# Conditioning weights asked for in two pairs, and three more merge additions on VectorE, in a decoder layer on one Trainium2 core

## The chip, the cores and the metric

The kernel runs on one core of one Trainium2 chip. The metric is device time in microseconds (us): the median of 3 runs of the unchanged kernel is 1647.31 (1646.59 to 1651.67).

## What is computed

One layer of a hybrid decoder, for a prompt of 1024 tokens and 8 samples of 8 tokens (1088 columns together; features stand in the 128 partitions), all in float32. Cut to what matters here:

```python
sh, sc, gt = ada_mod(c, w_ada_mix, b_ada_mix)
h = rms_norm(x, norm_mix) * (1 + sc) + sh
P = h @ w_in                                   # 34 blocks of 128 columns
...
merged = g_r * (o_r @ w_br_rwkv) + g_p * (o_p @ w_br_pool)
x = x + gt * (merged @ w_out)
sh, sc, gt = ada_mod(c, w_ada_mlp, b_ada_mlp)  # silu(c) @ w + b
h = rms_norm(x, norm_mlp) * (1 + sc) + sh
x = x + gt * (square(relu(h @ w_ff1)) @ w_ff2)
y = rms_norm(x, norm_final)
```

## The kernel before

Every large product is done with split operands: a weight piece of 128 x 512 (256 KB, tile `wraw`) is loaded by the SyncE queue (SP), rounded by ScalarE to `whi` (L207), and VectorE or GpSimd in turn forms the rest `wlo` (L208). TensorE then does three matmuls per 128-row slice (`mm3`). Raw buffers are two, so a load waits until the split of the piece two before it is done; rounded pieces are four deep in the second phase.

The first phase (to about 778 us of the span) projects, runs the recurrent and the pooling branch and stores the pooled half of the merge in DRAM. The second phase (`phase2`) begins with eight **merge rows** m = 0 to 7 (`or_job`): the last 512 rows of the recurrent branch are multiplied by `w_br` in three chunks of columns (two in PSUM tiles `mm`, one in `w`), VectorE multiplies each with the gate (L1406, into tile `t`), then the pooled part `u` (in a buffer of the tag `hid`) is added over all 1088 columns (L1410): on GpSimd for rows 0 to 6, on VectorE for row 7. ScalarE rounds the two halves of the sum to `mr` (L1413) and VectorE splits off the rest (L1414). Row 7's sum is also the mark for which the next stage waits.

Then come the eight **output blocks** (`out_job`), first for the left half of the columns, then for the right: each takes two pieces of `w_out`, 24 matmuls of 272 columns apiece, and ends in a residual step on VectorE (L1964), a store `d_xr` (L1448) and a square on ScalarE (L1450) that VectorE sums up (L1452). Blocks 0 and 1 are interleaved, so that the first two pieces need only merge rows 0 to 3.

Beside the output blocks the **conditioning of the MLP** is computed (`ada` in `phase2`, `ada_part`): of `w_ada_mlp` three parts g, of which g = 0 and 1 fall into this stage. Each has two groups of four loads of 512 KB into the four `hid` buffers (L305, on SP); 16 narrow matmuls `wc<-hid` consume a group. After the second group ScalarE copies the sum to `asb` (L311) and eight small matmuls `wc<-kct,asb` spread it. Before the four tiles of the very first group stands a GpSimd copy each of one column of merge row 7's sum (`behind`, L1379), so that the loads don't start before that sum is there.

What sets the order: TensorE's order is written by hand, by a pace (`Pace`) that adds up estimated times; a generator's `yield n` asks to go on n ns of that pace later. The other engines and the queues are ordered by the language's scheduler. Each engine and queue works strictly in its order, and a wait holds up all that stands behind it.

Of the kernel before, what the change touches and what calls it, by code (L numbers as in the profile page):

```python
# [13 lines left out]
ALU = mybir.AluOpType  # L14
# [136 lines left out]
class K:  # L151
# [144 lines left out]
    def ada_part(self, name, g, tile_of, sb, dst, bias, blocks, gap, turn=2000, lead=0, n=1):  # L296

        nc = self.nc
        ps = self.ps("wc")
        for k2 in range(0, 4, n):  # L300

            ws = []
            for i in range(2 * n):
                ws.append(tile_of())
                nc.sync.dma_start(ws[i], self.io[name][2 * k2 + i, g])  # L305
            yield gap if k2 else gap + lead
            for i in range(2 * n):
                for h in range(2):
                    q, k = 64 * (i % 2) + 32 * h, 2 * k2 + i
                    self.mm(ps[q:q + 32, :], self.sT[:, k, :], ws[i][:, h * 512:(h + 1) * 512], start=k < 2, stop=k > 5, tile_position=(0, q))  # L310
        nc.scalar.activation(sb, ps, AF.Copy)  # L311
        yield turn
        po = self.ps("wc")
        for i in range(4):
            self.mm(po[:, i * 18:(i + 1) * 18], sb[:, i * 128:(i + 1) * 128], self.kc("sel"), start=True, stop=True)
        b0, step = blocks[0], blocks[1] - blocks[0]
        pick = lambda t: t.rearrange("p (g h b) q -> p g h b q", h=2, b=4)[:, b0 // 8] if step == 4 else t.rearrange("p (h b) q -> p h b q", b=8)[:, 0:2, b0:b0 + 4]
        bb = pick(self.part[:, PC[bias]:PC[bias] + 24].unsqueeze(2))
        nc.vector.tensor_tensor(pick(dst), po[:, :72].rearrange("p (b h q) -> p h b q", h=2, q=9), bb.to_broadcast([P, 2, 4, 9]), op=ALU.add)
# [1046 lines left out]
    def phase2(self):  # L1366

        nc, io, p = self.nc, self.io, self.p2
# [8 lines left out]
        def behind(x):  # L1377

            nc.gpsimd.tensor_copy(x[:, 0:1], self.mark[:, 0:1])  # L1379
            return x  # L1380
# [17 lines left out]
        def or_job(m):  # L1398
            S = {}

            def begin():
                t, S["u"] = T(), self.row(p, "hid", 4)
                S["t"] = t
                nc.scalar.dma_start(t, self.d_th[m])
                nc.scalar.dma_start(S["u"], self.d_th[8 + m])
                return lambda c0, n, ps: nc.vector.scalar_tensor_tensor(t[:, c0:c0 + n], t[:, c0:c0 + n], 1.0, ps[:, :n], op0=ALU.add, op1=ALU.mult)  # L1406

            def after():
                t = S["t"]
                (nc.vector if m == 7 else nc.gpsimd).tensor_tensor(t, t, S["u"], op=ALU.add)  # L1410
                hi, lo = zip(*[MR() for _ in range(2)])
                for i, s in enumerate(split):
                    nc.scalar.activation(hi[i], t[:, s], AF.Copy)  # L1413
                    nc.vector.tensor_tensor(lo[i], t[:, s], hi[i].bitcast(F32), op=ALU.subtract)  # L1414
                mg[0].append(hi)
                mg[1].append(lo)
                self.mark = t
                self.xr.append(HX(F32))
                nc.gpsimd.dma_start(behind(self.xr[m]), io["xT"][m])
                self.done.add(("or", m + 4))  # L1420

            return Job([io["w_br"][m][:, 0:512]], begin, after=after, xs=lambda: orr, tags=TG)
# [672 lines left out]
```

## Time and profile before

| | |
|---|---|
| median of 3 runs | 1647.31 us |
| profiled execution | 1653.89 us, its span 1652.1 us |
| mean granted TensorE clock | 0.987 |
| merge rows and output blocks | about 778 to 945 us of the span |

The profile gives busy time by engine (PE is TensorE, PEld its weight loads, DVE VectorE, ACT ScalarE, POOL GpSimd, SP SyncE), and rows in order of time: start, length, engine, line, operation, tile written <- tiles read, shape and count; in brackets the idle time of the engine before it, and what ended it. A queue is marked by a q (SPq). DMA rows give the time of issuing, not of landing. The chain that ended last is the path of work and waits followed back from the end.

### The profile page before, as it was taken

How to read it: one execution, taken by the hardware profiler on the slowest of the kernel's cores; microseconds unless marked ns; L12 is line 12 of the kernel's file. 1: busy time of each engine (PE TensorE's matmuls, PEld its weight loads, DVE VectorE, ACT ScalarE, POOL GpSimd, SP SyncE). 2: the span in 40 equal slices, each digit the busy share in tenths (PEclk: the TensorE clock that was granted, in tenths of full speed). 3: DMA queues.
4: the chain of work that ended last, by engine and by line, in shares of the span. 5: the costliest groups of instructions: out<-in, count | busy, mean ns of one | idle time of the engine just before them, and what ended most of it. 6: DMA issues, size and time to landing. Idle time of an engine off the chain costs nothing.

```text
span 1652.1 us, 35483 instructions
## 1 busy us (share of the span) xinstructions
PE 1598.5 (97%) x14331; PEld 1492.5 (90%) x14331; DVE 1019.8 (62%) x1744; ACT 738.9 (45%) x1491; POOL 365.9 (22%) x467
## 2 busy tenths in 40 slices
PE   6999999999998999999989999999999999999997
PEld 3989888887897889889979999999999999999997
DVE  5675655745665456434543696777545677776866
ACT  4443343344334433423223475555444665553323
POOL 3300200010001000101621332323223342521221
PEclk9989999999999999999999999999999999999999
DMA  9324313314332323564875355666656965564213
GB/s 334 113 103 137 133 62 110 117 54 139 100 114 76 121 93 119 220 223 153 327 266 203 131 181 182 226 232 238 227 205 216 345 205 188 199 245 180 99 39 109
DMA packets 123332, 279.43 MB, mean 169 GB/s; under 512 B 16768, under 2 KB 31104, under 8 KB 123168
## 3 DMA queue, kind: packets, MB, share of 16 engines
q1 hardware_dynamic: 107808, 228.52, 39.6%
q0 software_dynamic: 9312, 32.41, 5.8%
q10 hardware_dynamic: 6048, 16.23, 2.7%
q8 instruction: 113, 1.85, 0.4%
q14 instruction: 51, 0.42, 0.1%
HBM read 198.15 MB, written 78.95 MB: 168 GB/s over the span
## 4 chain that ended last, share of the span: by engine, by line
PE 61%; ACT 2%; DVE 2%; DMA 2%; issue 1%; POOL 1%; SPq 0%; DVEq 0%; POOLq 0%; ACTq 0%
PE pr L184 32%; PE mm L184 21%; PE w L184 6%; PE wc L184 2%; DMA wraw<-in_w_out 1%; DVE hx L1772 0%; DMA wt<-d_x 0%; POOL t L1410 0%; PE w L191 0%; ACT whi L207 0%; DVE hx L1941 0%; POOL wr L1745 0%; ACT mr L1695 0%; ACT hx L1695 0%; DMA wraw<-in_w_ff 0%
## 5 line engine op out<-in xcount | busy, mean ns | idle before, releaser
L184 PE MATMUL mm<-hx,whi 128*128 128x362 f32 (+1 forms) x1920 | 510.0, 347 | 0.6 <-ACT px L551 0.6
L184 PEld LDWEIGHTS mm<-hx,whi 128*128 128x128 f32 x1920 | 333.3, 191 | 34.4 <-issue 17.1
L184 PE MATMUL pr<-mr,whi 128*128 128x272 f32 x1792 | 336.2, 287 | 0.3 <-DVE hx L1772 0.3
L184 PE MATMUL mm<-hx,wlo 128*128 128x362 f32 (+1 forms) x960 | 316.1, 329 | 0.0
L184 PEld LDWEIGHTS pr<-mr,whi 128*128 128x128 f32 x1792 | 280.7, 188 | 2.1 <-issue 1.3
L184 PE MATMUL pr<-mr,wlo 128*128 128x272 f32 x896 | 257.8, 288 | 0.0
L207 ACT ACTIVATE whi<-wraw 128x512 fp32r<-128x512 f32 x186 | 116.8, 629 | 217.9 <-PE mm L184 60.4
L184 PEld LDWEIGHTS mm<-hx,wlo 128*128 128x128 f32 x960 | 183.1, 191 | 0.0
L208 DVE TENSOR_TENSOR wlo<-wraw,whi 128x512 fp32r<-128x512 f32 x145 | 110.6, 764 | 116.5 <-ACT whi L207 114.0
L184 PE MATMUL pr<-hx,whi 128*128 128x272 f32 x896 | 168.8, 287 | 1.8 <-DVE rs L1967 0.8
L184 PEld LDWEIGHTS pr<-mr,wlo 128*128 128x128 f32 x896 | 168.6, 188 | 0.0
L184 PE MATMUL mm<-mr,whi 128*128 128x272 f32 (+4 forms) x736 | 154.3, 304 | 1.6 <-DVE t L1406 1.6
L184 PEld LDWEIGHTS pr<-hx,whi 128*128 128x128 f32 x896 | 140.3, 188 | 3.3 <-ACT whi L207 1.0
L207 ACT ACTIVATE whi<-wr 128x512 fp32r<-128x512 f32 x138 | 86.5, 628 | 117.3 <-PE pr L184 80.5
L184 PE MATMUL pr<-hx,wlo 128*128 128x272 f32 x448 | 128.9, 288 | 0.0
L184 PEld LDWEIGHTS mm<-mr,whi 128*128 128x128 f32 x736 | 120.7, 191 | 4.8 <-issue 2.5
L184 PE MATMUL mm<-mr,wlo 128*128 128x272 f32 (+4 forms) x368 | 111.0, 302 | 0.0
L208 POOL TENSOR_TENSOR wlo<-wraw,whi 128x512 fp32r<-128x512 f32 x41 | 54.8, 1336 | 216.3 <-ACT whi L207 216.3
L208 DVE TENSOR_TENSOR wlo<-wr,whi 128x512 fp32r<-128x512 f32 x103 | 77.2, 752 | 16.6 <-ACT whi L207 16.6
L184 PE MATMUL pr<-t,whi 128*128 128x272 f32 x448 | 84.6, 287 | 0.0
L184 PEld LDWEIGHTS pr<-hx,wlo 128*128 128x128 f32 x448 | 84.3, 188 | 0.0
L184 PEld LDWEIGHTS pr<-t,whi 128*128 128x128 f32 x448 | 70.2, 188 | 0.8 <-issue 0.8
(400 smaller groups left out, 2714.9 us busy)
## 6 DMA issues: line engine op xcount, KB each, us to landing
wr<-in_w_ff SPq DMA_DIRECT2D x137, 256.0 KB, 3.3
hid<-d_ch POOLq DMA_DIRECT2D x72, 272.0 KB, 3.7
wraw<-in_w_ff SPq DMA_DIRECT2D x71, 256.0 KB, 3.1
wraw<-in_w_in SPq DMA_DIRECT2D x68, 256.0 KB, 2.9
d_ch<-hx SPq DMA_DIRECT2D x52, 272.0 KB, 3.6
hid<-in_w_ada_mlp SPq DMA_DIRECT2D x24, 512.0 KB, 6.4
d_th<-px SPq DMA_DIRECT2D x22, 544.0 KB, 3.0
wt<-d_x SPq DMA_DIRECT2D x20, 544.0 KB, 4.2
```

What stands on the lines that cost most here:

```text
L184: return self.nc.tensor.matmul(out, lhsT, rhs, **kw)
L207: nc.scalar.activation(hi, raw, AF.Copy)
L208: (nc.gpsimd if pool else nc.vector).tensor_tensor(lo, raw, hi.bitcast(F32), op=ALU.subtract)
```

## The change

There are two edits. In `ada_part` a group of four loads (n = 2) is asked for in two pairs, with half of the gap between them, and the wait after the second pair is shorter by that half. Groups with n = 1 are as before. In `or_job` the addition of `u` is on VectorE for rows 4 to 7, where it was on VectorE for row 7 alone.

```diff
             ws = []
             for i in range(2 * n):
+                if i == 2:
+                    yield gap // 2
                 ws.append(tile_of())
                 nc.sync.dma_start(ws[i], self.io[name][2 * k2 + i, g])
-            yield gap if k2 else gap + lead
+            yield (gap if k2 else gap + lead) - (gap // 2 if n > 1 else 0)
...
             def after():
                 t = S["t"]
-                (nc.vector if m == 7 else nc.gpsimd).tensor_tensor(t, t, S["u"], op=ALU.add)
+                (nc.vector if m > 3 else nc.gpsimd).tensor_tensor(t, t, S["u"], op=ALU.add)
```

In the changed kernel all lines from L304 on stand two lower (L1410 is L1412, L207 and L208 stay).

**VectorE, merge rows 4 to 6.** `t_9045`, `t_9107`, `t_9169` and `t_9231` are rows 4, 5, 6 and 7; `mr` are their split halves; `wlo_9215` belongs to a piece of `w_out`. Before, from the end of row 5 to row 7:

```order
L1406 SCALAR_TENSOR_TENSOR t_9169<-t_9169,mm_9173 128x364
L1414 TENSOR_TENSOR mr_9160<-t_9107,mr_9160 128x544
L1406 SCALAR_TENSOR_TENSOR t_9169<-t_9169,mm_9174 128x362
L1406 SCALAR_TENSOR_TENSOR t_9169<-t_9169,w_9175 128x362
L1414 TENSOR_TENSOR mr_9161<-t_9107,mr_9161 128x544
L208 TENSOR_TENSOR wlo_9215<-wraw_9212,whi_9214 128x512
L1414 TENSOR_TENSOR mr_9222<-t_9169,mr_9222 128x544
L1406 SCALAR_TENSOR_TENSOR t_9231<-t_9231,mm_9235 128x364
L1406 SCALAR_TENSOR_TENSOR t_9231<-t_9231,mm_9236 128x362
L1414 TENSOR_TENSOR mr_9223<-t_9169,mr_9223 128x544
```

The same place in the changed kernel:

```order
L1416 TENSOR_TENSOR mr_9160<-t_9107,mr_9160 128x544
L1416 TENSOR_TENSOR mr_9161<-t_9107,mr_9161 128x544
L1408 SCALAR_TENSOR_TENSOR t_9169<-t_9169,mm_9173 128x364
L1408 SCALAR_TENSOR_TENSOR t_9169<-t_9169,mm_9174 128x362
L1408 SCALAR_TENSOR_TENSOR t_9169<-t_9169,w_9175 128x362
L1412 TENSOR_TENSOR t_9169<-t_9169,hid_9170 128x1088
L1416 TENSOR_TENSOR mr_9222<-t_9169,mr_9222 128x544
L1416 TENSOR_TENSOR mr_9223<-t_9169,mr_9223 128x544
L208 TENSOR_TENSOR wlo_9215<-wraw_9212,whi_9214 128x512
L1408 SCALAR_TENSOR_TENSOR t_9231<-t_9231,mm_9235 128x364
L1408 SCALAR_TENSOR_TENSOR t_9231<-t_9231,mm_9236 128x362
L1408 SCALAR_TENSOR_TENSOR t_9231<-t_9231,w_9237 128x362
```

The addition L1412 is new in VectorE's order, and a row's work is now closed before the next row's products begin; the split of a weight piece stands behind both halves of row 6.

**SP, from the second group of conditioning loads on.** `hid` are conditioning loads, `wraw` pieces of `w_out`, `d_xr` stores of a finished output block. Before:

```order
L196 DMA wraw_9483<-in_w_out 128x512
L305 DMA hid_9472<-in_w_ada_mlp 128x1024
L305 DMA hid_9474<-in_w_ada_mlp 128x1024
L305 DMA hid_9476<-in_w_ada_mlp 128x1024
L305 DMA hid_9478<-in_w_ada_mlp 128x1024
L196 DMA wraw_9513<-in_w_out 128x512
L196 DMA wraw_9551<-in_w_out 128x512
L1448 DMA d_xr_122<-hx_8980 128x544
L196 DMA wraw_9581<-in_w_out 128x512
L196 DMA wraw_9628<-in_w_out 128x512
L1448 DMA d_xr_123<-hx_9042 128x544
L305 DMA hid_9651<-in_w_ada_mlp 128x1024
```

And in the changed kernel:

```order
L196 DMA wraw_9479<-in_w_out 128x512
L307 DMA hid_9472<-in_w_ada_mlp 128x1024
L307 DMA hid_9474<-in_w_ada_mlp 128x1024
L196 DMA wraw_9509<-in_w_out 128x512
L307 DMA hid_9541<-in_w_ada_mlp 128x1024
L307 DMA hid_9543<-in_w_ada_mlp 128x1024
L196 DMA wraw_9551<-in_w_out 128x512
L1450 DMA d_xr_122<-hx_8980 128x544
L196 DMA wraw_9581<-in_w_out 128x512
L196 DMA wraw_9628<-in_w_out 128x512
L1450 DMA d_xr_123<-hx_9042 128x544
L196 DMA wraw_9670<-in_w_out 128x512
```

One piece of `w_out` now stands between the two pairs of this group, and one more stands ahead of the third group (as one does ahead of the fourth). In the first, third and fourth group the four loads still follow one another.

**ScalarE, around `asb`.** `whi` are rounded pieces of `w_out`, `t_9595` is the square of output block 3. Before:

```order
L207 ACTIVATE whi_9515<-wraw_9513 128x512
L207 ACTIVATE whi_9553<-wraw_9551 128x512
L1450 ACTIVATE t_9595<-hx_9042 128x544
L207 ACTIVATE whi_9583<-wraw_9581 128x512
L311 ACTIVATE asb_9298<-wc_9299 128x512
```

And in the changed kernel:

```order
L207 ACTIVATE whi_9511<-wraw_9509 128x512
L207 ACTIVATE whi_9553<-wraw_9551 128x512
L207 ACTIVATE whi_9583<-wraw_9581 128x512
L1452 ACTIVATE t_9595<-hx_9042 128x544
L313 ACTIVATE asb_9298<-wc_9299 128x512
```

The square and the third rounding have changed places; `asb` stands behind both as before.

## Prediction

> **What bounds the kernel now.** I read the page first, then the windows by stage, then the list of who waited for whom, then the order of time around each wait that TensorE (PE) shows.
>
> ```profile
> span 1652.1 us, 35483 instructions
> PE 1598.5 (97%) x14331; PEld 1492.5 (90%) x14331; DVE 1019.8 (62%) x1744; ACT 738.9 (45%) x1491; POOL 365.9 (22%) x467
> ```
>
> PE is busy for 97% of the span and VectorE (DVE) for 62%. A change that touches DVE, GpSimd (POOL) and the SyncE queue (SP) can therefore only gain where PE stands still, or lose where it makes PE stand still. The change sits in the merge and output stage, 778 to 945 us. The waits of PE from 700 to 960, and three windows there (columns: width, busy of PE, PEld, DVE, ACT, POOL, then granted clock, DMA share, GB/s):
>
> ```profile
> PE wc L184 <- ACT asb L311: 2.9, 1, 2.9
> PE mm L184 <- DVE t L1406: 1.6, 1, 1.6
> PE pr L184 <- DVE rs L1967: 0.8, 1, 0.8
> PE wc L184 <- DVE t L1452: 0.5, 1, 0.5
> ...
> 830.00:840.00 10.00, 10.00 (x81) 10.00 (x81) 7.03 (x11) 3.31 (x6) 4.31 (x8) 1.00 0.76 284
> ...
> 860.00:870.00 10.00, 7.09 (x36) 6.92 (x35) 2.90 (x6) 3.02 (x5) 1.27 (x1) 0.66 0.93 340
> ```
>
> Four waits, two of them large. After the 1.6 us one the clock stays at 1.00. Around the 2.9 us one only 36 matmuls run in 10 us and the granted clock is 0.66, so that wait costs more than its length. TensorE's rows at the two places, and four pieces of the chain that ended last, for the usual pace:
>
> ```profile
> 827.93 0.29 PE L184 MATMUL mm<-mr,wlo 128*128 128x272 f32 x1
> 829.84 0.49 PE L184 MATMUL mm<-mr,whi 128*128 128x272 f32 x2 [1.61 <-DVE t L1406]
> ...
> 859.88 0.29 PE L184 MATMUL mm<-mr,wlo 128*128 128x272 f32 x1
> 863.08 1.89 PE L184 MATMUL wc<-kct,asb 128*128 128x18 f32 x8 [2.91 <-ACT asb L311]
> 864.80 0.80 PE L184 MATMUL mm<-mr,whi 128*128 128x272 f32 x2
> ...
> 869.03 0.47 PE L184 MATMUL mm<-mr,whi 128*128 128x272 f32 x2
> ```
> ```profile
> 811.35 0.49 PE w L184 x3
> 811.84 1.00 PE mm L184 x6
> ...
> 897.64 0.80 PE wc L184 x8
> ...
> 902.08 31.39 PE mm L184 x252
> ```
>
> The usual pitch of a 272-column matmul is 31.39/252 = 0.125 us. **Place A:** from 827.93 + 0.125 to 829.84 PE loses 1.78 us. **Place B:** from 859.88 + 0.125 to 863.08 it loses 3.08. The eight small matmuls then take 864.80 - 863.08 = 1.72 instead of 0.80, 0.92 more; and the 18 matmuls between 864.80 and 869.03 (six groups of three) take 4.23 instead of 18 x 0.125 = 2.24, 1.99 more. B is 5.99 us, of which 2.91 is the slow clock. A and B together are 7.77 us.
>
> **What ends the wait at A.**
>
> ```profile
> 824.86 2.94 POOL L1410 TENSOR_TENSOR t<-t,hid 128x1088 f32<-128x1088 f32 x1
> 825.33 3.02 DVE L208 TENSOR_TENSOR wlo<-wraw,whi 128x512 fp32r<-128x512 f32 x1
> 828.52 0.73 DVE L1414 TENSOR_TENSOR mr<-t,mr 128x544 fp32r<-128x544 f32 x1 [0.17 <-ACT mr L1413]
> 829.16 0.97 DVE L1406 SCALAR_TENSOR_TENSOR t<-t,mm 128x364 f32<-128x364 f32 x2
> ...
> 831.98 1.29 DVE L1410 TENSOR_TENSOR t<-t,hid 128x1088 f32<-128x1088 f32 x1
> ```
>
> Merged row 6's addition runs on POOL until 827.80. DVE has the split of row 6 in its order ahead of the gated products of row 7 (L1406), so the two PSUM banks that the second output block needs come free only at 829.7. Besides, the weight split at 825.33 took 3.02 us, against 0.69 in a row below, and ended just after that addition. [...] The same addition on DVE (row 7, 831.98) took 1.29, less than half of POOL's 2.94.
>
> **Edit 2, the additions of rows 4 to 6 on DVE.** Row lengths for the schedule:
>
> ```profile
> 812.08 0.52 DVE L1406 SCALAR_TENSOR_TENSOR t<-t,w 128x362 f32<-128x362 f32 x1
> ...
> 816.35 0.72 DVE L1414 TENSOR_TENSOR mr<-t,mr 128x544 fp32r<-128x544 f32 x1 [3.12 <-ACT mr L1413]
> ...
> 818.96 0.69 DVE L208 TENSOR_TENSOR wlo<-wraw,whi 128x512 fp32r<-128x512 f32 x1
> ```
> ```profile
> 815.66 1.21 ACT L1413 ACTIVATE mr<-t 128x544 fp32r<-128x544 f32 x2 [4.79 <-POOL t L1410]
> ```
>
> By the new DVE order a row is: three products (about 0.45 apart, 1.4), addition 1.29, wait for ScalarE's first half (816.35 - 815.66 = 0.69), two splits (0.65 apart, 1.35), in two rows of three one weight split (0.69): 4.7 to 5.4 us. PE's row is 36 matmuls at (0.49 + 1.00)/9 = 0.165, 5.94 us, so DVE keeps up. Row 4's last product ends at 812.60 as before (row 3 still waits for POOL). From there: one split left, addition to 814.5, its splits to 816.5; row 5's products to 817.9, addition 819.1, weight split and splits 821.2; row 6's products 822.5, addition 823.8, splits 825.8, weight split 826.5; row 7's first product 827.0, last 827.9, addition 829.2. The first product of row 7 is then 2.7 us earlier than now, and 1.1 before PE wants it at 828.05: A goes. POOL still has two weight splits of 1.3 in this time (the chain's row at 857.68); if each held DVE up for 0.7, A keeps 0.3. I take 1.5 of A's 1.78 as gained.
>
> The addition of row 7 ends at 829.2 instead of 831.98 + 1.29 = 833.27: **4.1 us earlier**. Four POOL copies wait for it, and the first conditioning loads wait for those copies.
>
> **What ends the wait at B, and edit 1.** The SP queue, then the chain, then ScalarE and DVE:
>
> ```profile
> 834.06 1.77 SPq L305 DMA_DIRECT2D hid<-in_w_ada_mlp  x4
> 836.23 0.86 SPq L196 DMA_DIRECT2D wraw<-in_w_out  x2
> 837.19 2.79 SPq L1448 DMA_DIRECT2D d_xr<-hx  x2
> 846.36 0.33 SPq L196 DMA_DIRECT2D wraw<-in_w_out  x1
> 846.78 1.91 SPq L305 DMA_DIRECT2D hid<-in_w_ada_mlp  x4
> 848.79 2.15 SPq L196 DMA_DIRECT2D wraw<-in_w_out  x2
> ```
> ```profile
> 848.79 8.08 DMA wraw<-in_w_out
> ...
> 857.68 1.30 POOL wlo L208
> ...
> 859.00 2.81 DMA wraw<-in_w_out
> ```
> ```profile
> 856.97 1.29 ACT L207 ACTIVATE whi<-wraw 128x512 fp32r<-128x512 f32 x2 [4.88 <-DMA wraw<-in_w_out]
> ...
> 859.97 0.66 ACT L1450 ACTIVATE t<-hx 128x544 f32<-128x544 f32 x1 [1.70 <-DVE hx L1964]
> ...
> 861.91 0.63 ACT L207 ACTIVATE whi<-wraw 128x512 fp32r<-128x512 f32 x1 [1.29 <-DMA wraw<-in_w_out]
> 862.45 0.58 ACT L311 ACTIVATE asb<-wc 128x512 f32<-128x512 f32 x1
> ```
>
> The copy asb that PE waits for stands in ScalarE's order behind three weight roundings. The weights asked for behind the second group of four took 8.08 us to land where an unqueued one takes 2.81, so each 512 KB load ahead costs about (8.08 - 2.81)/4 = 1.3 us. Only after their split does a buffer come free for the weights of 859.00, the last rounding before asb.
>
> Edit 1 does less than its words: by the new SP order groups 1, 3 and 4 still stand four in a row; in group 2 one weight load moves between the pairs, and one goes ahead of group 3 and of group 4 each. TensorE's order stays but for a shift of one to three rows. So edit 1 takes two 512 KB loads, 2.6 us, from in front of one weight load.
>
> After both: group 1 and all behind it on SP move 4.1 earlier (846.36 to 842.3; the two stores at 837.19 to 839.98 in between wait for output blocks that PE finishes 1.5 earlier, so they don't bind). The weights now between the pairs are issued at 842.3 + 0.4 + 2 x 0.48 = 843.7 and land 8.08 - 2.6 = 5.5 later, 849.2; rounded and split 851.1; the next weights, issued then, land by 855 even behind the second pair, and are rounded by 855.7. The weights behind the second pair land as now less 4.1: their rounding, the second at 856.97, ends at 854.2, the DVE split at 854.9, two residual steps (0.5 each) 855.9, the square 856.6, asb 857.2. PE comes there at 860.0 - 1.5 = 858.5. **B goes whole, with 1.3 us to spare**; every us beyond that comes back as a wait. What is late next: the second pair itself, asked for at 844.1 to 845.0. It lands, by 1.3 a load and 2.8, by about 851, and PE reads it at 855.2 - 1.5. Later groups wait for PE itself to free the four buffers, and move with it.
>
> At nothing I cost: 3 x 1.29 = 3.9 us of DVE work, hidden under PE's rows as above (its price uncovered is the third rival), and 3 x 2.9 us less on POOL, which nobody waits for. Behind 945 us PE is busy throughout and its order is the same, so what is gained stays.
>
> **Sum:** 1.5 + 6.0 = 7.5 us. The profiled execution took 1653.89 us (1.8 around its span); it would take 1646.4. It stands 6.6 above the median of 1647.31, and the shown runs differ by 5.1, so B need not be the same in each. Taken from the median: **1639.8 us**.
>
> **Rivals.**
> *The clock part is not in the timed runs.* The drop followed a gap of 3.1 us and not one of 1.8, so it hangs on little. If the timed runs have the gap without the drop, the gain is 1.5 + 3.1 = 4.6: **1642.7**. For it: the median is so far under the profiled time. Against: the clock fell in the only row with so long a gap. [...]
> *The transfers set B.* DMA share is 0.93 in 860 to 870. If the loads cannot land 4.1 earlier, only the reordering helps: the weights behind the pairs land at 857.6 as now, so asb comes at about 861.5 and A's gain becomes a longer wait. Gain 1.5: **1645.8**, with nothing gained at 1647.3. Against: at 830 to 840 the share is 0.76, and SP's issue at 846.36 waits for a chain that begins with row 7's addition.
> *DVE becomes the bound.* Each row meets one POOL weight split of 1.3 us (that same row). If it held DVE for its whole 1.3 in each row, DVE's 5.4 would be 6.7, over PE's 5.94; from 0.5 us of hold-up per row on, PE waits for banks. Four rows lose 0.8 each, 3.1; row 7's addition comes no earlier, B stays, and one more slow clock of 2.9 may follow: 1647.31 + 6.0 = **1653.3**, or 1650.4 without the clock. For it: the 3.02 at 825.33. Against: that was behind a 2.94 us addition, which is gone.
>
> **Chances.** Forecast 0.56 (its own range 1637 to 1642.4); clock part absent 0.13; transfers 0.20; DVE the bound 0.11. The lower end lets the two small waits (0.8 and 0.5) and the 0.7 between median and fastest run go as well: 1639.8 - 0.3 - 2.0, about 1637. The upper end takes in the second rival but for its worst case: 1647. A change within 0.3%, 4.9 us, can hardly be told from none. Faster than 1642.4 holds the forecast and a third of the first rival, 0.60; slower than 1652.2 holds two thirds of the third, 0.07; between, 0.33.
>
> **What would show it.** In the changed profile: no wait of PE on L1406 near 828; the fourth row's to sixth row's additions on DVE at about 1.3; the first conditioning load near 830 instead of 834; asb before PE wants it, and a granted clock of 1.00 in the ten us that now have 0.66. It is wrong if DVE's additions take 2 us or more, if the weights behind the second pair still land near 857, or if PE waits for a second pair.

## The result, and the profile after

In six runs each the changed kernel took a median of **1641.57 us** (1637.99 to 1643.53) and the kernel before 1648.97 (1646.59 to 1652.95). The ratio is **0.9953**, 95% interval 0.9936 to 0.9969: 5.1 to 10.6 us faster, 7.75 in the middle (the ratio is not the quotient of the two medians, which lie 7.40 apart). Forecast were 1639.8 us and a gain of 7.5. The profiled execution took 1641.42 us.

The page of the kernel after:

```profile
span 1639.6 us, 35486 instructions
PE 1590.9 (97%) x14331; PEld 1486.2 (91%) x14331; DVE 1024.3 (62%) x1747; ACT 737.7 (45%) x1491; POOL 354.6 (22%) x464
```

DVE has 4.5 us more work and POOL 11.3 less, and neither shows in the end: PE is still the engine that is busy for 97%. What PE waited for from 700 to 960 us, after the change (us in total, times, longest):

```profile
PE pr L184 <- DVE rs L1969: 0.8, 1, 0.8
PE wc L184 <- DVE t L1454: 0.4, 1, 0.4
PE wc L184 <- ACT t L1452: 0.2, 1, 0.2
```

The 1.6 us for a gated product and the 2.9 for asb are gone. Two windows of after, which hold places A and B:

```profile
820.00:830.00 10.00, 10.00 (x80) 10.00 (x79) 6.55 (x10) 4.62 (x8) 4.65 (x10) 1.00 0.76 233
...
850.00:860.00 10.00, 10.00 (x84) 9.00 (x77) 5.93 (x9) 3.48 (x6) 2.58 (x2) 1.00 0.75 247
```

PE is busy for the whole of both, with 84 matmuls in the second and the clock at 1.00, where before had 36 and 0.66. VectorE's rows near A, after:

```profile
818.70 1.29 DVE L1412 TENSOR_TENSOR t<-t,hid 128x1088 f32<-128x1088 f32 x1
...
822.00 0.69 DVE L208 TENSOR_TENSOR wlo<-wraw,whi 128x512 fp32r<-128x512 f32 x1
822.60 0.97 DVE L1408 SCALAR_TENSOR_TENSOR t<-t,mm 128x364 f32<-128x364 f32 x2
...
824.04 1.29 DVE L1412 TENSOR_TENSOR t<-t,hid 128x1088 f32<-128x1088 f32 x1
```

The additions take 1.29 each, and the weight split that had taken 3.02 beside POOL's addition takes 0.69. The way to asb, after: SP's queue, then ScalarE, then PE.

```profile
825.73 1.91 SPq L307 DMA_DIRECT2D hid<-in_w_ada_mlp  x4
...
837.90 1.55 SPq L307 DMA_DIRECT2D hid<-in_w_ada_mlp  x2
839.56 0.37 SPq L196 DMA_DIRECT2D wraw<-in_w_out  x1
839.98 1.51 SPq L307 DMA_DIRECT2D hid<-in_w_ada_mlp  x2
```
```profile
846.01 0.63 ACT L207 ACTIVATE whi<-wraw 128x512 fp32r<-128x512 f32 x1 [2.77 <-DMA wraw<-in_w_out]
849.27 0.63 ACT L207 ACTIVATE whi<-wraw 128x512 fp32r<-128x512 f32 x1 [2.63 <-DMA wraw<-in_w_out]
...
852.12 0.58 ACT L313 ACTIVATE asb<-wc 128x512 f32<-128x512 f32 x1
```
```profile
853.86 0.96 PE L184 MATMUL wc<-kct,asb 128*128 128x18 f32 x8
```

asb is ready at 852.70 and PE comes for it at 853.86, 1.2 us later. The weight asked for between the pairs landed 6.3 us after its issue, one asked for behind both in 7.4.

**How the traces are compared.** The part ahead of the merge stage is the same code in all kernels, yet the merge products begin anywhere from 773.9 to 780.4 us in the executions below (before 778.35, after 774.67). The difference of two spans, 12.5 us here, therefore contains some microseconds that are not the change's. They go, at least in part, with the clock: ahead of the merge it stood at 0.50 for 17 to 20 us in the executions that begin the merge by 777.3, and for 24 to 27 us in those that begin it from 778.0 on. So I measure from the first output product (the first matmul that reads a merged row into an output block) to the first product that stands behind the residual, and call that **the stage**: 120.05 us before (825.06 to 945.11), 111.38 after (821.36 to 932.74), **8.67 less**. It is 1.78 at A, 5.99 at B, as priced from before's rows, and 0.9 besides: PE's first two groups of conditioning products took 2.66 and 2.13 before and 1.92 each after, because their loads came in time (the last loads of before's two groups landed 18.0 and 31.2 us behind the first output product, when PE had begun on the groups at 16.5 and 30.1).

The main executions, in us from the first output product (a plus sign in front of a time means the same from here on). "Again" is the same kernel in a further execution; the third column is the time from the first conditioning load's issue on SP to asb being ready (the end of ScalarE's copy).

| kernel | first load issued | asb ready | between | PE reads asb | stage |
|---|---|---|---|---|---|
| before | 9.00 | 37.97 | 28.97 | 38.02 | 120.05 |
| before, again | 8.55 | 36.74 | 28.19 | 36.79 | 117.84 |
| pairs alone | 7.92 | 34.51 | 26.59 | 35.08 | 114.19 |
| additions alone | 4.08 | 34.06 | 29.98 | 34.11 | 116.14 |
| additions alone, again | 3.63 | 32.70 | 29.07 | 32.75 | 113.31 |
| after | 4.37 | 31.34 | 26.97 | 32.50 | 111.38 |
| after, again | 3.94 | 30.96 | 27.02 | 32.50 | 111.24 |
| all additions on DVE | 4.24 | 32.88 | 28.64 | 33.03 | 114.56 |
| all additions, again | 4.03 | 31.12 | 27.09 | 32.50 | 111.01 |

Two things act on asb, and the columns part them. With the additions on DVE the first load is issued at 3.6 to 4.4 instead of 7.9 to 9.0. With the pairs the way from there takes 27.3 on the mean of five executions instead of 29.1 of four, 1.8 less. The further variants below agree: 26.8 to 27.2 in the four with pairs, 29.1 in the one without. The stages of one kernel differ by up to 3.6 us between two executions, so one profile alone does not settle a difference of that size.

### The profile page after: what moved, and what is told of

It is laid out like the page before. It is cut to its first block, busy times and chain, and to the rows that moved or that the text cites. A ratio compares the mean times of both kernels' runs of the same rounds, so it can differ in the third digit from the quotient of the medians.

```text
span 1639.6 us, 35486 instructions
## 1 busy us (share of the span) xinstructions
PE 1590.9 (97%) x14331; PEld 1486.2 (91%) x14331; DVE 1024.3 (62%) x1747; ACT 737.7 (45%) x1491; POOL 354.6 (22%) x464
## 4 chain that ended last, share of the span: by engine, by line
PE 87%; DVE 4%; ACT 3%; issue 3%; DMA 2%; POOL 1%; SPq 0%; DVEq 0%; POOLq 0%; ACTq 0%
PE mm L184 39%; PE pr L184 31%; PE w L184 12%; PE wc L184 4%; PE w L191 1%; DMA x<-in_xT 1%; DVE hx L1774 1%; DMA wraw<-in_w_out 0%; DMA wt<-d_x 0%; DVE wlo L208 0%; POOL wr L1747 0%; DVE hx L1943 0%; DMA d_y<-y 0%; ACT mr L1697 0%; DVE hx L1966 0%
## 5 line engine op out<-in xcount | busy, mean ns | idle before, releaser
L207 ACT ACTIVATE whi<-wraw 128x512 fp32r<-128x512 f32 x186 | 116.8, 628 | 218.5 <-PE mm L184 63.0
L208 DVE TENSOR_TENSOR wlo<-wraw,whi 128x512 fp32r<-128x512 f32 x145 | 107.1, 739 | 118.6 <-ACT whi L207 115.4
L207 ACT ACTIVATE whi<-wr 128x512 fp32r<-128x512 f32 x138 | 86.3, 627 | 111.4 <-PE pr L184 73.2
L208 POOL TENSOR_TENSOR wlo<-wraw,whi 128x512 fp32r<-128x512 f32 x41 | 55.1, 1345 | 212.1 <-ACT whi L207 212.0
L208 DVE TENSOR_TENSOR wlo<-wr,whi 128x512 fp32r<-128x512 f32 x103 | 76.2, 742 | 18.2 <-ACT whi L207 18.2
```

What stands on the lines that cost most here:

```text
L207: nc.scalar.activation(hi, raw, AF.Copy)
L208: (nc.gpsimd if pool else nc.vector).tensor_tensor(lo, raw, hi.bitcast(F32), op=ALU.subtract)
```

## The experiments

Theory going in: the two waits go because the row sums come earlier (edit 2), and edit 1 adds little. Rival: the pairs end the wait at B by themselves. Ratios are to the kernel before, run beside each variant. Lines that a variant adds move the line numbers behind them on.

**Pairs alone** (edit 2 undone).

```diff
-                (nc.vector if m > 3 else nc.gpsimd).tensor_tensor(t, t, S["u"], op=ALU.add)
+                (nc.vector if m == 7 else nc.gpsimd).tensor_tensor(t, t, S["u"], op=ALU.add)
```

> Edit 1 alone: the conditioning loads in two pairs, the additions of rows 4 to 6 on GpSimd as before. Measured by the stage from the first matmul on merged rows to the first matmul of the MLP, which took 120.05 us before and 111.38 after the change. My theory (the earlier sum of row 7 brings most of it, the pairs about 2.6 us of one weight load): place A keeps its 1.8 us, PE still waits for asb, but only 0.5 to 1.5 us and without the slow clock; stage 114.5 to 116, time about 4.5 us under before. Rival, that the pairs alone end the wait at B: stage 113.2 to 114.2. Rival, that one weight load moved does nothing: stage about 120 with a wait of 3 us and a granted clock near 0.66.

Measured: 1644.47 us median of 9 runs, ratio 0.9957 (0.9944 to 0.9971); stage 114.19. ScalarE's rows of this kernel:

```profile
848.99 0.63 ACT L207 ACTIVATE whi<-wraw 128x512 fp32r<-128x512 f32 x1 [1.67 <-DMA wraw<-in_w_out]
852.22 0.63 ACT L207 ACTIVATE whi<-wraw 128x512 fp32r<-128x512 f32 x1 [2.60 <-DMA wraw<-in_w_out]
...
855.01 0.58 ACT L313 ACTIVATE asb<-wc 128x512 f32<-128x512 f32 x1
```

Before, two weights were rounded together at 856.97, when both had landed; here the first is rounded 3.2 us ahead of the second, and its buffer is asked for anew at once. asb is ready at 855.59 and PE comes at 856.16: no wait. That is 3.5 earlier than before, 2.4 by the shorter way and 1.1 because the first load left SP that much sooner in this execution. Of the stage's 2.8 over after, 2.6 lie ahead of asb: a wait of 0.52 at A, and 1.8 in the first group of conditioning products, whose loads still come late (3.71 us instead of 1.92, with a wait of 0.75 inside). The rival holds in this execution: the pairs alone can end the wait. That A was 0.52, where my theory kept its 1.8, is not shown to come from the pairs: the additions stand on POOL as before, but row 6's began 1.3 us ahead of the first output product, and only 0.2 ahead of it before. In the second execution of before, where it began 0.6 ahead, A was 1.16. So A's size, too, moves from execution to execution.

**Additions alone** (edit 1 undone), in two executions.

```diff
-                if i == 2:
-                    yield gap // 2
...
-            yield (gap if k2 else gap + lead) - (gap // 2 if n > 1 else 0)
+            yield gap if k2 else gap + lead
```

> Edit 2 alone: additions of rows 4 to 6 on VectorE, conditioning loads four at once as before. Theory: A goes, row 7's sum comes about 4.2 us earlier as in the changed kernel, the weights behind the four loads land about 4.5 to 5 us earlier than before, asb is 0 to 1.5 us too late for PE, no slow clock; stage 111.4 to 113, time 6.5 to 8.5 us under before. Rival, that the pairs end the wait at B: stage about 118 (only A's 1.8 us gone), wait for asb over 3 us.

> The additions alone once more. If the missing 3 us are this kernel's own (four loads ahead of the weights behind the third group), the waits for asb (1.81) and for a squared residual (1.10) are there again and the stage takes 115.5 to 116.8. If they were one execution's landing times, the second wait can be gone and the stage is 113 to 114.

Measured: 1646.19 us median of 12 runs, ratio 0.9978 (0.9961 to 0.9996); stage 116.14 and 113.31 (the second execution, a single run, took 1648.67). PE's two waits in the first execution, and ScalarE's row ahead of the second:

```profile
854.68 1.07 PE L184 MATMUL wc<-kct,asb 128*128 128x18 f32 x8 [1.81 <-ACT asb L311]
...
876.93 1.35 PE L184 MATMUL wc<-kct,t 128*128 128x5 f32 x10 [1.10 <-DVE t L1452]
```
```profile
864.42 1.30 ACT L207 ACTIVATE whi<-wraw 128x512 fp32r<-128x512 f32 x2 [5.44 <-DMA wraw<-in_w_out]
```

A is gone, and PE stands ready for asb at +32.14, where before it did at 860.005 - 825.06 = +34.95. asb itself comes 3.9 earlier, but 2.8 of that is eaten by PE's own lead, and a wait of 1.81 stays. (In after PE reads asb at +32.50 because edit 1 has put three more products ahead of it, 0.37 us.) Later the weights behind the third group land for both of two roundings at once (the second row), and a squared residual is late. In the second execution the wait for asb is 0.45, and one of 1.03 for a residual's square on ScalarE (L1450) comes at +62, behind the fourth group: the weights behind its four loads were asked for at +51.5 and rounded at +59.5, and the square stands behind that rounding. My theory falls: the additions alone are worth 3.6 us (0.7 to 6.4) of the 7.75.

**The third group's loads at half their size**, on the additions alone: is that second wait made by the loads ahead of the weights?

```diff
-                nc.sync.dma_start(ws[i], self.io[name][2 * k2 + i, g])
+                w = 512 if name == "w_ada_mlp" and g == 1 and k2 == 0 else 1024
+                nc.sync.dma_start(ws[i][:, :w], self.io[name][2 * k2 + i, g][:, :w])
...
-                    self.mm(ps[q:q + 32, :], self.sT[:, k, :], ws[i][:, h * 512:(h + 1) * 512], start=k < 2, stop=k > 5, tile_position=(0, q))
+                    self.mm(ps[q:q + 32, :], self.sT[:, k, :], ws[i][:, h * 512 % w:h * 512 % w + 512], start=k < 2, stop=k > 5, tile_position=(0, q))
```

> The additions alone (four loads at once), with the four conditioning loads of the third group cut to half their columns; half of that group's products are made with the other half's weights, so that part of the result is left out. If the wait at +56 (1.10 for a squared residual, and the slow clock behind it) comes from the output weights that queue behind those four loads, they land 2 to 2.6 earlier, the wait goes, and the stage takes 112.8 to 113.8 instead of 116.14; the wait of 1.8 for asb stays. If it comes from the order on ScalarE and VectorE, it stays at 0.9 to 1.3 and the stage at 115.8 to 116.4.

Measured: 1644.24 us median of 10 runs, ratio 0.9963 (0.9943 to 0.9982); stage 112.64, a little under what was expected if the loads make the wait. The wait for the squared residual is gone, that for asb is 1.30:

```profile
864.23 0.63 ACT L207 ACTIVATE whi<-wraw 128x512 fp32r<-128x512 f32 x1 [5.07 <-DMA wraw<-in_w_out]
...
865.32 0.61 ACT L207 ACTIVATE whi<-wraw 128x512 fp32r<-128x512 f32 x1
```

Counted from the first output product (825.10 here, 820.57 there) this rounding starts at +39.1 instead of +43.9. The first weight behind the third group landed 4.6 us after its issue here, against 8.8 and 7.8 in the two executions with whole loads: the queued loads make these weights late. That they alone make the wait is not shown, because the second execution with whole loads had no such wait either, with the rounding at +41.5. In the changed kernel a weight goes ahead of that group instead; that this is what keeps the wait away there was not tried by itself.

**The additions of rows 6 and 7 only on VectorE**, with the pairs.

```diff
-                (nc.vector if m > 3 else nc.gpsimd).tensor_tensor(t, t, S["u"], op=ALU.add)
+                (nc.vector if m > 5 else nc.gpsimd).tensor_tensor(t, t, S["u"], op=ALU.add)
```

> The changed kernel with the additions of rows 4 and 5 back on GpSimd (rows 6 and 7 on VectorE), pairs kept. Theory: row 7's sum comes only 1.5 to 2 us earlier than before, A shrinks to 0.7 to 1.4 us, asb comes 0 to 0.8 us late or just in time, no slow clock; stage 112.5 to 113.8. If the wait at B hangs on the addition's place and not on how early the sum is, the stage is 111.4 as after the change; if it needs the full 4 us, the stage is 116 or more.

Measured: 1645.37 us median of 6 runs, ratio 0.9962 (0.9949 to 0.9976); stage 115.63, 1.8 over the forecast range. PE's waits at A:

```profile
826.97 0.49 PE L184 MATMUL mm<-mr,whi 128*128 128x272 f32 x2 [0.62 <-DVE t L1408]
...
828.97 0.82 PE L184 MATMUL mm<-mr,whi 128*128 128x272 f32 x2 [1.39 <-DVE t L1408]
```

With row 5 still on POOL, DVE stays behind through rows 6 and 7, and A is there, in two pieces. The clock then stood at 0.50 from 829.00 to 832.41, which at half speed costs 1.7 us more, an estimate, and the first conditioning products begin at +18.75 rather than +14.66. So A came to 2.01 us instead of 0.7 to 1.4, and a slow clock that I had ruled out came with it.

**GpSimd at work beside VectorE.** The changed kernel, with a POOL addition of about the old length (2.5 to 2.9) behind each DVE addition of rows 4 to 6, which nothing waits for.

```diff
                 (nc.vector if m > 3 else nc.gpsimd).tensor_tensor(t, t, S["u"], op=ALU.add)
+                if 3 < m < 7:
+                    nc.gpsimd.tensor_tensor(S["u"], t, S["u"], op=ALU.add)
```

> The changed kernel, and behind VectorE's addition of rows 4, 5 and 6 GpSimd adds the same two tiles into a buffer that nobody reads: nothing waits for it, it only runs beside VectorE. If the long GpSimd addition itself holds up VectorE (weight splits of 3 us instead of 0.7), VectorE loses about 2 us in two of the rows, PE gets a wait for a gated product of 1 to 2 us near row 7 again, the addition of row 7 ends 2 to 4 later and a wait for asb of 1 to 3 follows: stage 113 to 117 us. If only the order counted (the split standing behind a sum that was slow in coming), nothing moves: no such wait, 111.2 to 111.8.

Measured: 1651.49 us median of 10 runs, ratio 1.0006 (0.9986 to 1.0025); stage 118.73. DVE's rows, and PE's wait:

```profile
818.77 1.29 DVE L1412 TENSOR_TENSOR t<-t,hid 128x1088 f32<-128x1088 f32 x1
...
820.79 3.49 DVE L1418 TENSOR_TENSOR mr<-t,mr 128x544 fp32r<-128x544 f32 x2
...
827.66 3.09 DVE L1418 TENSOR_TENSOR mr<-t,mr 128x544 fp32r<-128x544 f32 x2 [0.72 <-ACT mr L1417]
830.67 2.19 DVE L208 TENSOR_TENSOR wlo<-wraw,whi 128x512 fp32r<-128x512 f32 x1
```
```profile
833.45 0.79 PE L184 MATMUL mm<-mr,whi 128*128 128x272 f32 x2 [5.34 <-DVE t L1408]
```

A row's two splits, which take 1.36 together in after, took 3.49 and 3.09 (of which the first split 2.85 and 2.45), and a weight split 2.19. The whole gain of the change is gone, through an operation whose result nobody reads. My price for this was low (a wait of 1 to 2; it was 5.34), since I had counted two rows held up and all three were; and the clock stood at 0.50 from 831.15 to 837.98, 4.5 us of it behind the wait, which at half speed costs 2.3 us more, an estimate. No wait for asb followed: PE was 7.7 us late already.

**The price of a wait for asb.** The changed kernel, with asb copied onto itself eight, or four, times on ScalarE before PE reads it, in the first group.

```diff
         nc.scalar.activation(sb, ps, AF.Copy)
+        for _ in range(8 if name == "w_ada_mlp" and g == 0 else 0):
+            nc.scalar.activation(sb, sb, AF.Copy)
```

> The changed kernel with eight more copies of asb in place on ScalarE (about 0.5 us each) before its small matmuls, in the first of the three conditioning parts only; the result is the same. It makes asb about 4 us later, against 1.2 us of slack in the trace, so PE waits about 3 us at B again, with nothing else of B's chain changed. Theory of the price: the wait's length plus about 2.9 us of slow clock behind it; stage 111.4 + 3 + 2.9 = 117.3. Rival, that the slow clock before came from something else: stage 114.3 with a granted clock of 1.00 behind the wait.

> The changed kernel with asb copied onto itself four times on ScalarE before PE reads it (first group only). With eight copies PE waited 4.41, of slack 1.2 and 8 x 0.70; four give 2.8 - 1.2 = 1.6. If the slow clock needs a lone wait longer than 1.8, it does not come: stage 111.38 + 1.6 = 113.0, clock 1.00 throughout. If any wait at this place brings it, 115.5 to 116, with matmuls near 0.23 behind the wait.

Measured: eight, 1650.29 us median of 10 runs, ratio 0.9997 (0.9982 to 1.0012), stage 118.67; four, 1644.46 of 10 runs, 0.9963 (0.9945 to 0.9981), stage 112.72. PE's row with eight copies, then with four:

```profile
859.68 0.61 PE L184 MATMUL wc<-kct,asb 128*128 128x18 f32 x2 [4.41 <-ACT asb L315]
```
```profile
858.54 1.07 PE L184 MATMUL wc<-kct,asb 128*128 128x18 f32 x8 [1.19 <-ACT asb L315]
```

The long wait costs the stage 7.29 over after: 4.41, and 2.88 that the slow clock accounts for (0.50 from 858.83 to 865.66). The short one costs 1.34, its length and little more. By the ratios they cost 7.3 and 1.6 us. For the long wait the timed runs follow the stage; for the short one the interval overlaps that of the change. Whether a threshold lies between the two is taken up in the last section.

**All eight additions on VectorE**, in two executions.

```diff
-                (nc.vector if m > 3 else nc.gpsimd).tensor_tensor(t, t, S["u"], op=ALU.add)
+                nc.vector.tensor_tensor(t, t, S["u"], op=ALU.add)
```

> All eight rows' additions on VectorE, pairs kept. My theory: additions of rows 0 to 3 hold up nothing that PE waits for (after the change PE shows no wait for a merge product), and the slack before asb is already there; the stage takes 111.2 to 111.6 us as after the change and the timed ratio is that of the change, 0.995. The rival, VectorE becomes the bound: four more additions of 1.29 in the merge part put waits on the gated products, and the part from the first merge product to the first output product takes over 47.2 instead of 46.7.

> All eight additions on VectorE once more. Its first profile had a wait of 1.38 us for a squared residual at +55, behind weights that landed later than after the change although the queue has the same order. If that is the kernel's own, it is there again with 1.0 to 1.7 and the stage takes 114 to 115 us. If it is the landing times of one execution, the wait is another and the stage can be 111.2 to 112.

Measured: 1642.36 us median of 12 runs, ratio 0.9953 (0.9935 to 0.9971), the change's own; merge part 46.68, as in after. The stage took 114.56 in the first execution, with a wait of 1.38 for a squared residual at +55, and 111.01 in the second, a single run of 1645.52, without it. That wait goes with the landing times of one execution and not with the order of the queue: the way from the first load to asb took 28.64 in the one and 27.09 in the other, with the queue in the same order. PE's row:

```profile
876.60 1.25 PE L184 MATMUL wc<-kct,t 128*128 128x5 f32 x10 [1.38 <-DVE t L1454]
```

So the first of the two forecasts for the repetition falls, and the rival (VectorE as the bound) in both.

**Before and after once more.**

> The kernel before once more, for the spread of the profiled stage (first output product to the first product behind the residual). If the readings of one execution can be trusted to half a microsecond, it takes 119.5 to 120.6 us again, with the wait for asb at 2.6 to 3.2 and the slow clock behind it. If transfers land differently from execution to execution, the wait for asb moves by 1 us or more and the stage by that or, without the slow clock, by 3 to 6.

> The changed kernel once more. If the readings repeat: stage 111.2 to 111.8 us, no wait for asb and none for a squared residual. If landing times vary by 1 us or more: asb ends between +30 and +33 where it ended at +31.3, and a wait for a squared residual near +55 can appear, stage up to 115.

Measured, one run each: 1652.83 and 1642.69 us (a further run of before beside them took 1655.67), stages 117.84 and 111.24, so **6.60** less in this pair against 8.67 in the first. After repeats to 0.14; before does not. Before's waits, and the window around its wait for asb:

```profile
PE wc L184 <- ACT asb L311: 1.9, 1, 1.9
PE wc L184 <- ACT t L1450: 1.3, 1, 1.3
PE mm L184 <- DVE t L1406: 1.2, 1, 1.2
```
```profile
860.00:870.00 10.00, 8.05 (x66) 7.83 (x65) 3.55 (x7) 3.02 (x5) 1.27 (x1) 1.00 0.94 335
```

asb was ready 1.2 earlier, PE waited 1.95, and the clock did not fall at all; further on PE waited 1.31 for a residual's square (L1450), which it did not in the first execution. Both places are there in each execution, and the slow clock at B in one of two.

## Why the prediction was right, step by step

**The sum was right, and its two halves were weighed wrongly.** 7.5 us were forecast; the runs gave 7.75 (5.1 to 10.6), the two pairs of profiles 8.67 and 6.60. That the sum came out so near is in part luck: it counts a slow clock that one of two executions of before has, and leaves out the late first groups that both have.

- *Place A, 1.5 of 1.78.* All of it went: no gated product is waited for in either execution of after. (1.78 was one execution's; A's wait was 1.61 there and 1.16 in the second.) POOL's remaining weight splits, 1.40 at 817.10 and 1.48 at 822.37, held DVE up in none of rows 4 to 7 of after: the two gated products beside each took 0.97, as at 812.52 with none beside them. Four splits of `mr` on DVE that began while such a POOL split of 1.28 to 1.30 ran did take longer: 1.35 at 806.44, in row 3 of after, and 1.36, 1.12 and 1.45 at 810.36, 822.77 and 830.05 of before, against 0.72 at 816.35. So the 0.7 for each that the forecast set against A lies at the upper end of what these rows show, 0.4 to 0.7, but in rows 4 to 7 nothing of the kind came. (In the run with rows 6 and 7 only, a weight split on DVE took 1.74 beside one.) That the old POOL addition held DVE up was argued from one split of 3.02; the POOL additions put back beside DVE show it, with pairs of splits of 3.09 and 3.49 and a stage 7.35 longer.
- *Row 7's sum 4.1 earlier, and with it SP's queue.* Its end stood 8.21 behind the first output product before and 3.97 after: 4.24 earlier. The first conditioning load left SP at +4.4 instead of +9.0.
- *B goes whole with 1.3 to spare.* It went, and 1.2 were left. Two errors cancel in that: asb ended at +31.3 where the schedule had it at +32.1, and PE came at +32.5 where the schedule had it at +33.4, because the first groups took 0.9 us less and all of A went, while the three more products cost 0.37.
- *"Edit 1 does less than its words."* As to asb its size was near: 2.6 us were taken from in front of one weight load, and the way to asb is 1.8 shorter. What I made of it was wrong, as my expectations for the two halves show. With the additions alone PE comes as early as in after, and the missing 1.8, with the 0.37 of the three products, turns the 1.2 to spare into waits of 1.81 and 0.45. With the pairs alone PE is still held up at A and comes later, so there the wait could go too.
- *What is late next.* **This step holds for the change as a whole, and fails for its halves.** I priced the second pair alone, and let later groups move with PE. With the additions alone the weights behind the third group are late in one execution and those behind the fourth in the other; for the third the run with half-size loads shows that the loads ahead make its weights late. The single weights that edit 1 puts ahead of these groups I had counted for nothing. With both edits the step holds, but with little to spare: the second pair landed by +27.1, with PE reading it from +27.9, and a wait behind the third group was there in one execution of all additions on DVE.
- *A term missing:* the 0.9 us inside PE's first two groups of conditioning products, whose loads were late before.
- *Rivals.* "The clock part is not in the timed runs" is not borne out: before has it in one of two profiled executions, and the timed runs speak for it on the average, since the rest of the kernel is the same code. The mean granted clock is 0.9907 over 61 timed runs of before, 0.9923 over the six of the changed kernel and 0.9917 over the twelve of all additions on DVE; 0.0010 to 0.0016 of 1650 us is 1.7 to 2.6 us, an estimate, where 2.9 was priced. The forecast time is 1.8 under the median measured, and 1.7 of that is the kernel before, which took 1648.97 in this comparison and 1647.31 in the runs that the forecast started from. "The transfers set B" is out as a bound: the first load is issued 4.6 earlier and the way from it to asb is no longer than before. "DVE becomes the bound" did not happen, and the run beside a busy POOL shows what it would have cost.

Open is what the earlier start of the conditioning loads is worth by itself: a kernel that has both edits and delays only these loads was not run. Nor do the timed runs separate pairs alone (0.9944 to 0.9971) from the full change (0.9936 to 0.9969); that the additions add to the pairs rests on the profiled stages, 114.19 against 111.38 and 111.24, of which the first is one execution. It is likely and not shown. No version beat the changed kernel.

## What to carry to other kernels

When a wait is taken from the busiest engine, work out when it now comes to its next wait: it arrives earlier by what was gained, and a producer that moves by less gives the gain back there. A load that is asked for between others also brings forward the load that waits for its buffer; here the way from the first load to asb became 1.8 us shorter. And before a stage is priced to the microsecond, profile the kernel a second time: here the same code gave 120.05 and 117.84.

## What was not expected of the hardware

The clock's fall does not follow the length of the wait. Waits of 1.95 (before, again), 1.81 (additions alone), 1.61 (A of before), 1.31, 1.19 and 1.03 left it at 1.00; a wait of 1.38 (all additions), one of 1.10 (additions alone) and the two of 0.62 and 1.39 (rows 6 and 7 only) brought it to 0.50. The 1.38 and the 1.10 were each followed by ten matmuls of 1 to 5 columns that last 1.25 to 1.35 us, but so were the 1.31 and the 1.03, by ten of one column. So the run with four copies, which fitted a threshold of about 2 us, shows no threshold. The windows of 2 us behind the 1.38 (all additions):

```profile
877.00:879.00 2.00, 2.00 (x17) 2.00 (x17) 0.06 (x1) 0.00 (x0) 0.00 (x0) 0.90 0.95 326
879.00:881.00 2.00, 2.00 (x11) 2.00 (x11) 0.73 (x2) 0.00 (x0) 0.00 (x0) 0.50 0.98 378
881.00:883.00 2.00, 2.00 (x14) 2.00 (x14) 0.28 (x1) 0.04 (x1) 0.00 (x0) 0.75 1.05 408
```

The traces of before and after have no granted clock but 1.00 and 0.50, so a window's share of slow clock is (1 - clock) / 0.5: these three add up to 0.4 + 2.0 + 1.0 = 3.4 us of half speed. Around B of before the clock stood at 0.50 from 862.32 to 869.15, 6.8 us, twice as long.

The traces show what the fall goes with. In before, and in after, all falls begin on one grid of 3.413 us: in before those at 316.18, 381.04, 507.33 and 862.32 lie 64.86, 126.29 and 354.99 us apart, which is 19, 37 and 104 steps, and the clock stays at 0.50 for 3.41, 3.41, 6.83 and 6.83 us, one step or two. Where a wait lies on that grid differs from execution to execution. Here are the step that holds the wait and the step behind it, for B of before, B of before again, the 1.10 and the 1.03 of the additions alone, and the 0.62 with the 1.39 (the second number is PE's busy time, and the clock is the third from the end):

```profile
858.91:862.32 3.41, 1.26 (x10) 1.04 (x9) 1.75 (x3) 1.06 (x2) 0.06 (x1) 1.00 0.59 187
862.32:865.73 3.41, 2.65 (x12) 2.65 (x13) 0.99 (x2) 1.33 (x3) 1.27 (x1) 0.50 1.00 362
...
859.87:863.28 3.41, 1.78 (x15) 1.56 (x13) 1.11 (x2) 1.50 (x3) 0.14 (x1) 1.00 0.86 258
863.28:866.69 3.41, 3.09 (x25) 3.09 (x26) 1.32 (x3) 0.85 (x2) 1.13 (x1) 1.00 0.91 340
...
874.53:877.94 3.41, 2.31 (x21) 2.12 (x19) 1.36 (x1) 0.86 (x2) 1.28 (x1) 1.00 0.94 334
877.94:881.35 3.41, 3.41 (x17) 3.41 (x17) 0.00 (x0) 0.00 (x0) 0.00 (x0) 0.50 1.00 359
...
887.05:890.46 3.41, 2.38 (x25) 1.17 (x17) 1.51 (x3) 2.44 (x5) 1.27 (x1) 1.00 0.37 134
890.46:893.87 3.41, 3.41 (x30) 3.41 (x30) 0.88 (x2) 1.66 (x3) 0.00 (x0) 1.00 0.80 260
...
825.59:829.00 3.41, 1.40 (x11) 0.99 (x9) 3.41 (x6) 0.99 (x2) 1.27 (x1) 1.00 0.53 171
829.00:832.41 3.41, 3.41 (x15) 3.41 (x16) 1.71 (x3) 0.71 (x2) 1.23 (x6) 0.50 0.59 169
```

B of before put 2.15 us of idle time into one step, and the clock fell at its end; B of before again was split over two steps, 1.63 and 0.32, and it did not. If the ten small matmuls are counted as idle, PE was idle for 2.01 to 3.41 us in the step ahead of each of the six falls of this stage, and for at most 2.00 us in every step that no fall followed. No run tried this count by itself.
